# A two-layer decoder trunk: the MLP's down projection with tokens on the partitions, and a changed order of first loads

## The chip, the cores and the metric

One of the eight cores of a Trainium2 chip. The metric is the device time of one execution in microseconds (us), the median of several runs. In the profile PE is TensorE's matmuls, PEld its weight loads, DVE VectorE, ACT ScalarE, POOL GpSimd, SP the engine that only issues DMAs. L155 is line 155 of the kernel before.

## The reference

The trunk has 256 tokens, a model width of 2048, and two layers. Each layer is a mixer and a gated MLP, each behind an RMS norm and with a residual. Layer 0's mixer joins a gMLP (8 head groups) and a gated recurrence (HGRN2, 8 heads); layer 1's is an attention with forget gates (16 heads). The part that the change touches most is the MLP's last product:

```python
def conv_ffn(h, w_up, conv_w, conv_b, w_down):
    z = h @ w_up                                   # (256, 2048) x (2048, 2 * 5632)
    zp = jnp.pad(z, ((0, 0), (CONV_WIDTH - 1, 0), (0, 0)))
    z = sum(conv_w[j] * zp[:, j:j + seq] for j in range(CONV_WIDTH)) + conv_b
    a, b = jnp.split(z, 2, axis=-1)
    return (jax.nn.silu(a) * b) @ w_down           # (256, 5632) x (5632, 2048)

for l in range(DEPTH):
    x = x + mixer(rms_norm(x, mix_norm[l]))
    x = x + conv_ffn(rms_norm(x, ffn_norm[l]), ...)
```

Everything is float32 in and out.

## The kernel before

**Layout.** The residual stream x is held with features on the partitions: 16 tiles xT[m] of 128 features x 256 tokens. All weights stream from memory once, about 430 MB.

**Split products.** Every large product is computed from float32 values cut in two: a high part rounded to the matmul's fast format (fp32r) and the rest. ScalarE makes the high part wh of a weight tile (L139), VectorE the rest wl (L141), from the raw tile w that SP's queue loads (L137); all in weights(). Activations are split likewise by split(): one tile of 512 columns holds 256 columns high, 256 low. A product is high x high + low x high + high x low.

**Two forms of projection.** project() keeps features on the partitions: per weight tile of 128 x 128 one matmul with wh against all 512 columns (L155) and one with wl against the 256 high columns (L158), both into one PSUM bank; fold() or add_x() add the two halves. The argument run says how many weight tiles are taken together before the order changes from wh to wl. project_tok() puts tokens on the partitions: the activation is the stationary operand and 512 columns of weights stream past; three matmuls (L177, L178, L179) per weight tile row and half of the tokens, into two banks. It serves v, i and the attention's q, k, v.

**Small work between.** Generators (hgrn, attend, mixes, gated, spatial, finish) do the recurrence, the attention and other small parts; tick() is called once per weight load and advances every generator in flight by one yield; depth[0] is how many may be in flight (2). They use PSUM banks from px, the projections those of pm. The order of instructions on each engine is written down ahead of time by a list scheduler from the program's order and its dependencies.

**Norm.** feed_split(k) makes the split, gain-scaled tile a of xT[k]; feed_square(k) adds its square to acc. At the kernel's start both run inside the first project_tok, the adds on POOL. Elsewhere feed() does both, on VectorE, right after a tile of x is complete. finish() makes the row factor R.

**Start.** The 2 MB of x come as five parts, the first by SP's queue, four by ScalarE's; the first 100 columns of the parameter array pp come by POOL's queue; WARM matmuls on a tile of ones run meanwhile.

**MLP.** ffn() goes over 4 groups of 11 hidden tiles. up(g) makes a group's 11 activations from 22 projections (conv); down(g) adds the group's product into all 16 tiles of x: per tile m one project() over 11 hidden tiles in chunks of 6 and 5, then add_x. The order is up 0, up 1, down 0, up 2, down 1, up 3, down 2, down 3. In down 3 each finished tile goes to feed() (layer 0) or to the output (layer 1). A second weight pool (fw) makes the buffers deeper during the MLP.

Of the kernel before, what the change touches and what calls it, by code (L numbers as in the profile page):

```python
# [14 lines left out]
P = 128  # L15
# [6 lines left out]
HT = HID // P  # L22
GRP = 11
EPS = 1e-6
WARM = 12
LEVELS = (64, 32, 16, 8, 4, 2, 1)
NL = len(LEVELS)
MCOLS = 2 * (NL + 1) * P
# [16 lines left out]
def tile_trunk(ctx: ExitStack, tc: tile.TileContext, x, pp_d, cst_d, mlev_d, msk_d,  # L45
# [5 lines left out]
    wp = ctx.enter_context(tc.tile_pool(name="wp", bufs=4))  # L51
    apool = ctx.enter_context(tc.tile_pool(name="ap", bufs=KT))
    tp = ctx.enter_context(tc.tile_pool(name="tp", bufs=2))
    pm = ctx.enter_context(tc.tile_pool(name="pm", bufs=3, space=bass.MemoryType.PSUM))
    px = ctx.enter_context(tc.tile_pool(name="px", bufs=1, space=bass.MemoryType.PSUM))

    count = [0]
# [1 line left out]
    def nm(base):  # L59
        count[0] += 1  # L60
        return f"{base}_{count[0]}"

    xT = []
    xload = []
    for c0, n in ((0, 2), (2, 2), (4, 4), (8, 4), (12, 4)):
        t = cp.tile([P, n, S], F32, tag=f"x{c0}", name=f"x{c0}")
        xload.append((t, c0, n))
        xT += [t[:, i] for i in range(n)]
    pp = cp.tile([P, NPP], F32, tag="pp", name="pp")
    cst = cp.tile([P, NK], F32, tag="cst", name="cst")  # L70
    ones = cp.tile([P, P], F32, tag="ones", name="ones")
    one1 = cp.tile([P, 1], F32, tag="one1", name="one1")

    nc.gpsimd.dma_start(pp[:, 0:C_CW], pp_d[:, 0:C_CW])
    V.memset(ones, 1.0)
    V.memset(one1, 1.0)
    ident = cst[:, K_ID:K_ID + P]
# [23 lines left out]
    def bank(tag="px"):  # L101
        n = nm(tag)
        return px.tile([P, 512], F32, tag=tag, name=n, bufs=banks[tag])

    banks = {"px": 5}
    flight, queue = [], []

    def tick():
# [6 lines left out]
    depth = [2]  # L115

    SC.preload_act_table_set(LNEXP)
    for i, (t, c0, n) in enumerate(xload):
        (SC if i else nc.sync).dma_start(t, x[:, c0:c0 + n, :])
    warm = pm.tile([P, 512], F32, tag="pm", name="warm")  # L120
    for i in range(WARM):
        PE.matmul(warm[:, 0:P], ones, ones, start=True, stop=True)
# [1 line left out]
    def drain():  # L124
        while flight or queue:
            tick()

    deep = {"pool": None, "turn": 0}

    def weights(src, n):  # L130
        deep["turn"] += 1
        if deep["pool"] is not None and deep["turn"] > 6 and deep["turn"] % 2:
            pool, nw, ns = deep["pool"], 4, 2
        else:
            pool, nw, ns = wp, 4, 3
        w = pool.tile([P, n], F32, tag="w", name=nm("w"), bufs=nw)
        nc.sync.dma_start(w, src)  # L137
        wh = pool.tile([P, n], F32R, tag="wh", name=nm("wh"), bufs=ns)
        SC.activation(wh, w, AF.Copy)  # L139
        wl = pool.tile([P, n], F32R, tag="wl", name=nm("wl"), bufs=ns)  # L140
        V.tensor_tensor(wl, w, wh.bitcast(F32), ALU.subtract)  # L141
        return wh, wl

    def project(wsrc, acts, chunks=(8, 8), k0=0, run=1):
        ps = pm.tile([P, 512], F32, tag="pm", name=nm("pm"))
        nk = sum(chunks)
        done = 0
        for c in chunks:
            lo = (k0 + done) * P
            tick()  # L150
            wh, wl = weights(wsrc[:, lo:lo + c * P], c * P)
            for k1 in range(0, c, run):
                ks = range(k1, min(k1 + run, c))
                for k in ks:
                    PE.matmul(ps, wh[:, k * P:(k + 1) * P], acts[done + k],  # L155
                              start=done + k == 0, stop=False, skip_group_check=True)
                for k in ks:
                    PE.matmul(ps[:, S:2 * S], wl[:, k * P:(k + 1) * P], acts[done + k][:, 0:S],  # L158
                              start=False, stop=done + k == nk - 1, skip_group_check=True)
            done += c  # L160
        return ps

    def project_tok(wsrc, norm, feed=False):
        ps = [pm.tile([P, 512], F32, tag="pm", name=nm("pm")) for _ in range(2)]
        k = 0
        for c in ((1, 1, 1, 1) + (2,) * 6 if feed else (2,) * 8):
            if feed:
                for i in range(c):
                    norm.feed_split(k + i)
            tick()  # L170
            wh, wl = weights(wsrc[:, k * 512:(k + c) * 512], c * 512)
            for T in range(2):
                for i in range(c):
                    a = norm.a[k + i]
                    ah, al = a[:, T * P:(T + 1) * P], a[:, S + T * P:S + (T + 1) * P]
                    h, l = (t[:, i * 512:(i + 1) * 512] for t in (wh, wl))
                    PE.matmul(ps[T], ah, h, start=k + i == 0, stop=False)  # L177
                    PE.matmul(ps[T], ah, l, start=False, stop=False)  # L178
                    PE.matmul(ps[T], al, h, start=False, stop=k + i == KT - 1)  # L179
            if feed:  # L180
                for i in range(c):
                    norm.feed_square(k + i, nc.gpsimd)
            k += c
        return ps

# [3 lines left out]
        V.tensor_tensor(t, ps[:, 0:S], t, ALU.add)  # L189
        return t  # L190

    def project_norm(wsrc, acts, R, out=None, run=1):
        t = fold(project(wsrc, acts, run=run))
        if out is None:
            out = t
        V.tensor_tensor(out, t, R, ALU.mult)  # L196
        return out
# [72 lines left out]
    def mixer_ab(norm):  # L270
# [10 lines left out]
        gv, late = [], []  # L281

        def finish():
            yield
            late.extend(norm.finish(tok=True))
            yield
            for T in range(2):
                act(gv[0][:, T], gv[0][:, T], AF.Gelu, scale=late[1][:, T:T + 1])
# [14 lines left out]
        A = norm.a  # L303

        SC.dma_start(cst, cst_d)
        wt = hp.tile([P, 2, NH, P], F32, tag="QK", name="wt", bufs=2)
        SC.dma_start(wt[:, 0], spw_d)
        SC.dma_start(wt[:, 1], spb_d.partition_broadcast(P))
        SC.dma_start(pp[:, C_CW:NPP], pp_d[:, C_CW:NPP])
# [63 lines left out]
        for h in range(NH):  # L373
# [9 lines left out]
            lf.append(l)  # L383
            kq.append(t)
        yB = [None] * KT

        itoks = []

        def hgrn(h):
            l, t = lf[h], kq[h]  # L390
            d0 = (h % 4) * P
            SC.activation(l, l, AF.Identity, bias=lb[:, h:h + 1], scale=omlb[:, h:h + 1])
            st = hp.tile([P, 2, P], F32, tag="st", name=nm("st"), bufs=2)
            dg = bank()
            for T in range(2):
                PE.matmul(dg[:, T * P:(T + 1) * P], t[:, T], t[:, 3 - T], start=True, stop=True)  # L396
# [2 lines left out]
            yield  # L399

            V.tensor_tensor(t[:, 2:4], t[:, 2:4], view(l, P, (-P, 2), (1, P)), ALU.mult)
            E = hp.tile([P, NL, 2, P], F32, tag="QK", name=nm("E"), bufs=2)
            tot = l
            for li in reversed(range(NL)):
                n = LEVELS[li]
# [17 lines left out]
            for c0, c1 in ((0, 4), (4, NL)):  # L423
                sps = bank()
                for li in range(c0, c1):
                    PE.matmul(sps[:, (li - c0) * P:(li - c0 + 1) * P],  # L426
                              E[:, li, 0], E[:, li, 1], start=True, stop=True)
                if c0 == 0:
                    xps = bank()
                    PE.matmul(xps[:, 0:P], t[:, 0], t[:, 2], start=True, stop=True)  # L430
                    s128 = hp.tile([P, P], F32, tag="s128", name=nm("s128"), bufs=2)
                    SC.activation(s128, xps[:, 0:P], AF.Copy)
                V.tensor_tensor(smk[:, c0 * P:c1 * P], sps[:, 0:(c1 - c0) * P],
                                msk[:, c0 * P:c1 * P], ALU.mult)
                for li in range(c0, c1):
                    n = LEVELS[li]
                    sv = view(st[:, 1], 0, (2 * n, 64 // n), (n - P, 2), (1, n))
                    V.tensor_tensor(sv, sv, smk[:, li * P:(li + 1) * P].rearrange(
                        "p (b two n) -> p b two n", two=2, n=n), ALU.add)
# [59 lines left out]
        for h in range(NH):  # L499
# [10 lines left out]
            if gates and not (queue or flight):  # L510
                queue.extend(spatial(b, z) for b, z in todo)
                todo = []
        drain()

        nxt = Norm(C_FFN)
        ks = [yB[8 + h] for h in range(NH)] + [yB[h] for h in range(NH)]
        for m in range(KT):
            add_x(m, project(w_abo[m], ks, run=4))
            nxt.feed(m)
        es.close()  # L520
        return nxt
# [2 lines left out]
    def mixer_c(norm):  # L524
# [109 lines left out]
            todo = []  # L634
        nxt = Norm(C_FFN + KT)
        for m in range(KT):
            add_x(m, project(w_co[m], yB, run=4))
            nxt.feed(m)
        es.close()
        return nxt  # L640
# [2 lines left out]
    def ffn(l, norm, last):  # L643
# [5 lines left out]
        nxt = None if last else Norm(C_MIX + KT)  # L649

        def conv(j):
            z = project_norm(w_up[l, j], A, R, run=(2, 8)[l])

            def w(i):
                c = C_CW + (l * 3 + i) * 2 * HT + j
                return pp[:, c:c + 1]

            cb = C_CB + l * 2 * HT + j
            c = hp.tile([P, S], F32, tag="conv", name=nm("conv"), bufs=4)
            SC.activation(c, z, AF.Identity, bias=pp[:, cb:cb + 1], scale=w(2))  # L660
            V.scalar_tensor_tensor(c[:, 1:], z[:, :S - 1], w(1), c[:, 1:], ALU.mult, ALU.add)  # L661
            V.scalar_tensor_tensor(c[:, 2:], z[:, :S - 2], w(0), c[:, 2:], ALU.mult, ALU.add)  # L662
            return c

        def up(g):
# [9 lines left out]
                hid.append(t)  # L675
            return hid

        def down(g, hid):
            for m in range(KT):
                add_x(m, project(w_dn[l, m], hid, chunks=(6, 5), k0=g * GRP, run=(3, 6)[l]))  # L680
                if g == HT // GRP - 1:
                    if last:
                        nc.sync.dma_start(out[:, m, :], xT[m])
                    else:
                        nxt.feed(m)

        hids = [up(0)]
        for g in range(HT // GRP):
# [91 lines left out]
```

## Time and profile before

| | us |
|---|---|
| time, median of 3 runs (2371.09 to 2371.52) | 2371.42 |
| the profiled execution's own time | 2372.19 |
| its span, first to last instruction | 2370.4 |

| engine | busy us | share of the span | instructions |
|---|---|---|---|
| PE | 2360.5 | 100% | 13118 |
| PEld | 2045.7 | 86% | 13118 |
| DVE | 1754.6 | 74% | 2969 |
| ACT | 1324.8 | 56% | 2249 |
| POOL | 16.2 | 1% | 20 |

The costliest groups of instructions, with the mean of one: the weight splits of 128 x 1024 take 1.06 us on ScalarE (640 of them) and 1.23 us on VectorE; those of 128 x 768 and 128 x 640 (the down projection's) 0.85 and 0.74 us on ScalarE, 0.96 and 0.83 us on VectorE. The adds of a 128 x 256 tile on VectorE take 0.41 to 0.43 us, of 128 x 512 0.69 us. The DMA engines were busy 45% to 75% of most stretches, at 185 GB/s on average. The granted clock of TensorE was 0.998 of full speed over the span.

How to read it: busy shares of TensorE count a matmul from its start to its modelled end, and matmuls overlap, so the distance between the starts of neighbours says more than a duration. Idle time of an engine that is not the bottleneck costs nothing.

### The profile page before, as it was taken

The page shows a single profiled execution, that of the slowest core. Times are in us where ns is not written, and L with a number is a line of the kernel's source. Part 1 is how long each engine was busy: PE and PEld are TensorE (multiplying, and loading weights), DVE is VectorE, ACT ScalarE, POOL GpSimd, SP SyncE. Part 2 cuts the span into 40 slices and gives each one's busy share as a digit, 9 for nine tenths or more (in the row PEclk, how much of TensorE's full clock was granted, in tenths as well). Part 3 has the DMA queues.
Part 4 walks back from the last instruction along what each step waited for, and adds up shares of the span by engine and source line. Part 5 has one row for each costly group of instructions (what it writes and reads, how often), then busy time and mean ns, then how long its engine had stood idle before and what let it go on. Part 6 is the DMA issues. An engine that isn't in the chain of part 4 may idle for free.

```text
span 2370.4 us, 35641 instructions
## 1 busy us (share of the span) xinstructions
PE 2360.5 (100%) x13118; PEld 2045.7 (86%) x13118; DVE 1754.6 (74%) x2969; ACT 1324.8 (56%) x2249; POOL 16.2 (1%) x20
## 2 busy tenths in 40 slices
PE   9999999999999999999999999999999999999999
PEld 7888888888888888888888888888888888888888
DVE  7778886878767867867766666767778767767765
ACT  6655665655555555556555455556555555555543
POOL 2000000000000000000000000000000000000000
PEclk9999999999999999999999999999999999999999
DMA  7554455655575566566656554557555575575565
GB/s 259 178 167 153 152 190 202 223 191 190 156 211 198 167 193 206 172 174 187 198 170 182 171 161 167 187 189 238 194 187 187 155 223 189 153 222 189 153 190 145
DMA packets 133727, 439.69 MB, mean 185 GB/s; under 512 B 14865, under 2 KB 16929, under 8 KB 133425
## 3 DMA queue, kind: packets, MB, share of 16 engines
q1 hardware_dynamic: 132224, 433.40, 58.2%
q10 hardware_dynamic: 1296, 3.97, 0.5%
q8 instruction: 104, 1.70, 0.3%
q14 instruction: 71, 0.57, 0.1%
q0 software_dynamic: 32, 0.05, 0.0%
HBM read 435.24 MB, written 2.11 MB: 185 GB/s over the span
## 4 chain that ended last, share of the span: by engine, by line
PE 97%; DVE 2%; ACT 1%; issue 0%; DMA 0%; ACTq 0%; DVEq 0%; POOLq 0%
PE pm L155 53%; PE pm L158 27%; PE pm L178 5%; PE pm L177 5%; PE pm L179 5%; DVE wl L141 1%; PE px L426 1%; PE px L599 0%; PE px L563 0%; PE px L570 0%; DMA pp<-in_pp 0%; PE px L594 0%; DVE a L205 0%; PE px L396 0%; ACT wh L139 0%
## 5 line engine op out<-in xcount | busy, mean ns | idle before, releaser
L141 DVE TENSOR_TENSOR wl<-w,wh 128x1024 fp32r<-128x1024 f32 (+3 forms) x900 | 1015.8, 1129 | 519.2 <-ACT wh L139 513.4
L139 ACT ACTIVATE wh<-w 128x1024 fp32r<-128x1024 f32 (+3 forms) x900 | 883.2, 982 | 904.4 <-PE pm L155 635.1
L155 PE MATMUL pm<-a,wh 128*128 128x512 f32 x3600 | 1074.7, 395 | 0.0
L158 PE MATMUL pm<-a,wl 128*128 128x256 f32 x3600 | 694.5, 281 | 0.0
L155 PEld LDWEIGHTS pm<-a,wh 128*128 128x128 f32 x3600 | 614.9, 189 | 79.4 <-DVE a L205 0.8
L158 PEld LDWEIGHTS pm<-a,wl 128*128 128x128 f32 x3600 | 604.6, 189 | 76.5 <-issue 0.2
L155 PE MATMUL pm<-hid,wh 128*128 128x512 f32 x1408 | 389.0, 394 | 0.0
L155 PEld LDWEIGHTS pm<-hid,wh 128*128 128x128 f32 x1408 | 239.3, 189 | 27.9
L158 PEld LDWEIGHTS pm<-hid,wl 128*128 128x128 f32 x1408 | 219.8, 189 | 33.6
L158 PE MATMUL pm<-hid,wl 128*128 128x256 f32 x1408 | 228.9, 281 | 0.0
L177 PE MATMUL pm<-wh,a 128*128 128x512 f32 x512 | 203.8, 399 | 3.0 <-ACT wh L139 3.0
L178 PE MATMUL pm<-wl,a 128*128 128x512 f32 x512 | 201.9, 394 | 0.9 <-DVE wl L141 0.9
L179 PE MATMUL pm<-wh,a 128*128 128x512 f32 x512 | 201.1, 393 | 0.0
L177 PEld LDWEIGHTS pm<-wh,a 128*128 128x128 f32 x512 | 96.9, 189 | 22.5 <-ACT wh L139 3.2
L178 PEld LDWEIGHTS pm<-wl,a 128*128 128x128 f32 x512 | 96.9, 189 | 21.5 <-DVE wl L141 2.5
L179 PEld LDWEIGHTS pm<-wh,a 128*128 128x128 f32 x512 | 96.8, 189 | 20.0
L660 ACT ACTIVATE conv<-ev,pp 128x256 f32<-128x256 f32 x176 | 103.1, 586 | 18.2 <-DVE ev L196 18.1
L189 DVE TENSOR_TENSOR ev<-pm,ev 128x256 f32<-128x256 f32 x225 | 93.8, 417 | 4.2 <-ACT ev L188 4.2
L661 DVE SCALAR_TENSOR_TENSOR conv<-ev,pp,conv 128x255 f32<-128x255 f32 x176 | 84.2, 478 | 8.7 <-ACT conv L660 8.7
L662 DVE SCALAR_TENSOR_TENSOR conv<-ev,pp,conv 128x254 f32<-128x254 f32 x176 | 85.0, 483 | 6.2
L188 ACT ACTIVATE ev<-pm 128x256 f32<-128x256 f32 x225 | 82.5, 366 | 0.7 <-PE pm L158 0.6
L196 DVE TENSOR_TENSOR ev<-ev,R 128x256 f32<-128x256 f32 x184 | 78.2, 425 | 6.1
(176 smaller groups left out, 1453.5 us busy)
## 6 DMA issues: line engine op xcount, KB each, us to landing
w<-in_w_up SPq DMA_DIRECT2D x352, 512.0 KB, 4.2
w<-in_w_dn SPq DMA_DIRECT2D x128, 384.0 KB, 3.2
w<-in_w_cqkv SPq DMA_DIRECT2D x96, 512.0 KB, 3.7
w<-in_w_dn SPq DMA_DIRECT2D x128, 320.0 KB, 3.3
w<-in_w_abo SPq DMA_DIRECT2D x32, 512.0 KB, 3.5
w<-in_w_cg SPq DMA_DIRECT2D x32, 512.0 KB, 3.8
w<-in_w_co SPq DMA_DIRECT2D x32, 512.0 KB, 3.6
w<-in_w_f SPq DMA_DIRECT2D x16, 512.0 KB, 4.5
```

Of the source, the lines that this page charges most:

```text
L139: SC.activation(wh, w, AF.Copy)
L141: V.tensor_tensor(wl, w, wh.bitcast(F32), ALU.subtract)
L155: PE.matmul(ps, wh[:, k * P:(k + 1) * P], acts[done + k], start=done + k == 0, stop=False, skip_group_check=True)
L158: PE.matmul(ps[:, S:2 * S], wl[:, k * P:(k + 1) * P], acts[done + k][:, 0:S], start=False, stop=done + k == nk - 1, skip_group_check=True)
L177: PE.matmul(ps[T], ah, h, start=k + i == 0, stop=False)
L178: PE.matmul(ps[T], ah, l, start=False, stop=False)
L179: PE.matmul(ps[T], al, h, start=False, stop=k + i == KT - 1)
L188: SC.activation(t, ps[:, S:2 * S], AF.Copy)
L189: V.tensor_tensor(t, ps[:, 0:S], t, ALU.add)
L660: SC.activation(c, z, AF.Identity, bias=pp[:, cb:cb + 1], scale=w(2))
L661: V.scalar_tensor_tensor(c[:, 1:], z[:, :S - 1], w(1), c[:, 1:], ALU.mult, ALU.add)
L662: V.scalar_tensor_tensor(c[:, 2:], z[:, :S - 2], w(0), c[:, 2:], ALU.mult, ALU.add)
```

## The change

1. The down projection. Groups and order stay. For each group the 16 output tiles are taken in four quarters of four tiles. A quarter has tokens on the partitions: two PSUM banks (one per half of the tokens), the hidden activation as stationary operand, and 512 columns of weights, four tiles m side by side, as moving operand, three matmuls per hidden tile and half. A weight load takes two hidden tiles of four m (128 x 1024, the last one of a quarter 128 x 512), in runs of 1 KB instead of 3 and 2.5 KB. The sums are collected over groups in y (128 x 2 x 2048). In the last group turn() transposes y's tiles back, four f32 transposes per bank and eight per quarter, and adds them to x; the last quarter of the last group is done by project() as before.
2. First loads: x in seven parts, each issued beside the k-tile of the first project_tok where FETCH puts it (parts from tile 8 on by ScalarE's queue, the others by SP's); the first 32 columns of pp by SP, ahead of everything, the next 68 by ScalarE after cst; 15 warming matmuls; the first norm's squares leave the first project_tok and go into finish(), on VectorE.
3. run=2 in every project().
4. Three heads in flight in the recurrence (depth 3, one more yield at hgrn's start, own buffers E, three of st and s128); four banks each in pm and px instead of 3 and 5.

```diff
-WARM = 12
+WARM = 15
+FETCH = {0: (0,), 1: (1, 2, 8), 2: (4, 6), 3: (12,)}
...
-    pm = ... bufs=3 ...
+    pm = ... bufs=4 ...
-    for c0, n in ((0, 2), (2, 2), (4, 4), (8, 4), (12, 4)):
+    for c0, n in ((0, 1), (1, 1), (2, 2), (4, 2), (6, 2), (8, 4), (12, 4)):
...
-    nc.gpsimd.dma_start(pp[:, 0:C_CW], pp_d[:, 0:C_CW])
+    nc.sync.dma_start(pp[:, 0:C_FFN], pp_d[:, 0:C_FFN])
...
-    banks = {"px": 5}
+    banks = {"px": 4}
...
-    for i, (t, c0, n) in enumerate(xload):
-        (SC if i else nc.sync).dma_start(t, x[:, c0:c0 + n, :])
...
-    def project(wsrc, acts, chunks=(8, 8), k0=0, run=1):
+    def project(wsrc, acts, chunks=(8, 8), k0=0, run=2):
...  project_tok
             if feed:
+                for c0 in FETCH.get(k, ()):
+                    t, c0, n = fetch[c0]
+                    (SC if c0 >= 8 else nc.sync).dma_start(t, x[:, c0:c0 + n, :])
                 for i in range(c):
                     norm.feed_split(k + i)
...
-            if feed:
-                for i in range(c):
-                    norm.feed_square(k + i, nc.gpsimd)
...  mixer_ab
         def finish():
-            yield
+            for k in range(KT):
+                norm.feed_square(k)
+                if k % 3 == 2:
+                    yield
             late.extend(norm.finish(tok=True))
...
         SC.dma_start(cst, cst_d)
+        SC.dma_start(pp[:, C_FFN:C_CW], pp_d[:, C_FFN:C_CW])
...
+        depth[0] = 3
         def hgrn(h):
+            yield
-            st = ... bufs=2 ...
+            st = ... bufs=3 ...
-            E = hp.tile([P, NL, 2, P], F32, tag="QK", name=nm("E"), bufs=2)
+            E = hp.tile([P, NL, 2, P], F32, tag="E", name=nm("E"), bufs=2)
...
-            add_x(m, project(w_abo[m], ks, run=4))
+            add_x(m, project(w_abo[m], ks, run=2))
...
-            z = project_norm(w_up[l, j], A, R, run=(2, 8)[l])
+            z = project_norm(w_up[l, j], A, R, run=2)
...  ffn
+        y = hp.tile([P, 2, D], F32, tag="y", name=nm("y"))
+        def turn(m0):
+            for m in range(m0, m0 + 4, 2):
+                tps = bank()
+                for i in range(4):
+                    PE.transpose(tps[:, i * P:(i + 1) * P],
+                                 y[:, i % 2, (m + i // 2) * P:(m + i // 2 + 1) * P], ident)
+                for i in range(2):
+                    V.tensor_tensor(xT[m + i], xT[m + i], tps[:, i * S:(i + 1) * S], ALU.add)
+        def finish_x(m):
+            if last:
+                nc.sync.dma_start(out[:, m, :], xT[m])
+            else:
+                nxt.feed(m)
         def down(g, hid):
-            for m in range(KT):
-                add_x(m, project(w_dn[l, m], hid, chunks=(6, 5), k0=g * GRP, run=(3, 6)[l]))
-                if g == HT // GRP - 1:
-                    if last:
-                        nc.sync.dma_start(out[:, m, :], xT[m])
+            final = g == HT // GRP - 1
+            late = []
+            for q in range(4):
+                if final and q == 3:
+                    for m in range(4 * q, KT):
+                        ps = project(w_dn[l, m], hid, chunks=(6, 5), k0=g * GRP, run=2)
+                        if late:
+                            late.pop()()
+                            turn(4 * q)
+                        add_x(m, ps)
+                        finish_x(m)
+                    return
+                ps = [pm.tile([P, 512], F32, tag="pm", name=nm("pm")) for _ in range(2)]
+                for k in range(0, GRP, 2):
+                    c = min(2, GRP - k)
+                    lo = (g * GRP + k) * P
+                    wh, wl = weights(w_dn[l, 4 * q:4 * q + 4, :, lo:lo + c * P]
+                                     .rearrange("m p c -> p m c"), 4 * c * P, 4)
+                    for T in range(2):
+                        for i in range(c):
+                            a = hid[k + i]
+                            ah, al = a[:, T * P:(T + 1) * P], a[:, S + T * P:S + (T + 1) * P]
+                            h, lo_ = (view(t, i * P, (c * P, 4), (1, P)) for t in (wh, wl))
+                            PE.matmul(ps[T], ah, h, start=k + i == 0, stop=False)
+                            PE.matmul(ps[T], ah, lo_, start=False, stop=False)
+                            PE.matmul(ps[T], al, h, start=False, stop=k + i == GRP - 1)
+                    if k == 4 and late:
+                        late.pop()()
+                for T in range(2):
+                    d = y[:, T, q * 512:(q + 1) * 512]
+                    if g == 0:
+                        SC.activation(d, ps[T], AF.Copy)
                     else:
-                        nxt.feed(m)
+                        V.tensor_tensor(d, d, ps[T], ALU.add)
+                if final:
+                    def done(m0=4 * q):
+                        turn(m0)
+                        for m in range(m0, m0 + 4):
+                            finish_x(m)
+                    late.append(done)
```

## The prediction

> **What bounds the kernel now.** I read the page first, then the idle time by waits, then TensorE's own timeline stage by stage, because only that shows what one matmul really takes from start to start.
>
> From the page (parts 1, 4 and 6) and the view of waits:
>
> ```profile
> span 2370.4 us, 35641 instructions
> PE 2360.5 (100%) x13118; PEld 2045.7 (86%) x13118; DVE 1754.6 (74%) x2969; ACT 1324.8 (56%) x2249; POOL 16.2 (1%) x20
> ...
> PE 97%; DVE 2%; ACT 1%; issue 0%; DMA 0%; ACTq 0%; DVEq 0%; POOLq 0%
> ...
> pp<-in_pp POOLq DMA_DIRECT2D x1, 50.0 KB, 6.3
> ```
>
> ```profile
> ACT wh L139 <- PE pm L155: 635.1, 584, 3.1
> ```
>
> TensorE fills 97% of the chain. ScalarE's largest wait is for TensorE to give a weight buffer back, so the weights are made ahead of need. Only two things can move the time: fewer nanoseconds of TensorE issue, or a new hole in its stream. A mean duration (395 ns for a 512-column matmul) is latency; what counts is the distance between starts. Four excerpts of TensorE's timeline (start, us, line, tiles, count):
>
> ```profile
> 1205.20 0.39 PE L177 MATMUL pm<-wh,a 128*128 128x512 f32 x1
> 1205.42 0.39 PE L178 MATMUL pm<-wl,a 128*128 128x512 f32 x1
> 1205.65 0.39 PE L179 MATMUL pm<-wh,a 128*128 128x512 f32 x1
> 1205.88 0.39 PE L177 MATMUL pm<-wh,a 128*128 128x512 f32 x1
> ```
>
> ```profile
> 1700.42 2.00 PE L155 MATMUL pm<-a,wh 128*128 128x512 f32 x8
> 1702.26 1.11 PE L158 MATMUL pm<-a,wl 128*128 128x256 f32 x8
> 1703.21 2.00 PE L155 MATMUL pm<-a,wh 128*128 128x512 f32 x8
> ```
>
> ```profile
> 2250.43 1.55 PE L155 MATMUL pm<-hid,wh 128*128 128x512 f32 x6
> 2251.82 0.88 PE L158 MATMUL pm<-hid,wl 128*128 128x256 f32 x6
> 2252.53 1.32 PE L155 MATMUL pm<-hid,wh 128*128 128x512 f32 x5
> 2253.70 0.76 PE L158 MATMUL pm<-hid,wl 128*128 128x256 f32 x5
> 2254.29 0.40 PE L155 MATMUL pm<-hid,wh 128*128 128x512 f32 x1
> ```
>
> ```profile
> 1216.08 1.03 PE L563 MATMUL px<-cst,z 128*128 128x128 f32 x8
> 1216.87 0.48 PE L177 MATMUL pm<-wh,a 128*128 128x512 f32 x1
> 1217.19 0.40 PE L178 MATMUL pm<-wl,a 128*128 128x512 f32 x1
> ```
>
> First: with tokens on the partitions (project_tok) a 512-column matmul starts every 227 ns. Second and third: with features on the partitions (project) a weight tile costs one 512- and one 256-column matmul: (1703.21-1700.42)/8 = 349 ns in the up projection, (2254.29-2250.43)/11 = 351 ns here; over whole down groups (61.65 us for 176 pairs in each of four) 350.3 ns. At 227 ns per 512 columns those 768 columns would take 340. Fourth: eight f32 transposes take 0.79 us and the next matmul runs 0.09 us late, 0.88 in all.
>
> **The change, part by part**, against the profiled execution: 2372.19 us, a span of 2370.4 and 1.8 around it, 0.8 above the median of 2371.42.
>
> Down projection. Per four output tiles and one hidden tile, 4 x 350.3 = 1401 ns become 6 matmuls x 227 = 1360 ns. Of 1408 (m,k) pairs the last quarter of the last group of each layer (2 x 44) stays as it was, so 1320 x (350.3-340) = **-13.6 us**. No row shows a moving operand in four runs of 128 columns at a stride, as these weight views are. Two 256-column matmuls (113 to 120 ns each) cost about one of 512, so a break has no fixed price there: I take 227. The other end is 233, the start distance of 512-column matmuls inside project, which leaves no gain.
>
> Transposes. Four calls of turn() per layer, eight transposes each: 8 x 0.88 = **+7.0 us** on TensorE, with nothing to hide them (ends 6.4, at 0.8 per turn, and 8).
>
> The Trainium skill (TensorE: Matmul & The Clock Gate, Part 4) says that transposes do not count as activity for the full clock. If so, 0.8 us of them every 15 us could cost clock; the attention stage, which holds such bursts, kept a granted clock of 1.00, so the trace does not bear out a price.
>
> VectorE and ScalarE in the down groups. Per quarter VectorE has 5 x 1.23 + 0.69 (splits) + 2 x 0.69 (adds into y) = 8.2 us against TensorE's 15.0; before it was 4 x (1.78+0.84) = 10.5. Cost nothing. In layer 0's last group feed() and turn() come in bursts of four tiles: 8.2 + 4 x (0.42+0.98) = 13.8 of 15.0, and at the last four tiles 4 x 3.6 + 5.6 + 1.7 = 21.7 us of VectorE against 17 of TensorE. Five split buffers (10 us of work) cover part; what is late is the last normalised tile, for which the next projection already waited a little. **+1 us** (0 to 5). The two last turn() calls need four px banks, and there are four.
>
> Weight loads of the down groups are 512 KB in 1 KB runs instead of 384 and 320 KB in 3 and 2.5 KB runs, one per 12 x 227 = 2.72 us (193 GB/s). The 2064 packets of 1024 B in this trace (mostly the output stores) took 46.8 ns on average: 512 x 46.8 / 16 = 1.5 us per load. Hidden; if not, see the first rival.
>
> Runs of two. Layer 0's up projection already has run=2: 348.3 ns per pair (122.61 us for 352). Layer 1's (run 8) takes 349.2, w_co (4) 350.8, w_abo (4) 353.4. Run 1 falls at 346.7 or 353.8, by stretch. To 348.3: 1408 x 0.9 + 256 x 2.5 + 256 x 5.1 = 3.2; the 784 pairs of run 1 about 1 (w_cg alone sits at 353.8). As w_abo's price may come from its tiles, not its run, I take **-3.6** (+1 to -5).
>
> Start. The first real matmul starts at 8.65 us, because pp comes by the POOL queue at 1.23 + 6.3, and then a split (0.51) and wh (0.61) follow. Two stretches (busy and count of PE, PEld, DVE, ACT, POOL; clock; DMA share; GB/s):
>
> ```profile
> 8.65:14.80 6.15, 6.15 (x15) 4.75 (x16) 5.82 (x10) 5.46 (x13) 2.91 (x3) 0.50 1.00 361
> 14.80:34.40 19.60, 18.75 (x80) 14.46 (x79) 19.01 (x19) 17.00 (x32) 12.39 (x12) 1.00 0.64 185
> ```
>
> In the first TensorE had half its clock after an idle 3 us, and the DMA engines were full; in the second VectorE was, slowed by the squares on POOL (a split of 0.86 beside POOL, 0.48 without). After: pp is first on SP (16 KB by SP took 3.6 us elsewhere, so 4.3), x0 one and w0 two issues of 0.4 behind it; w0 at about 5.5, first matmul about 6.2, where 30 warming matmuls end. x1 and x2 go ahead of w1 on SP, x4 and x6 ahead of w2, two 512 KB parts on ScalarE's queue. Up to w3 that is 3.1 MB, 8.5 us at 361 GB/s, so TensorE still waits at k=1 to 3 and has four of 16 k-tiles by about 13; the other 72 matmuls take 16.3 us: end near 30 instead of 34.4. The 16 squares and 15 adds (16 x 0.40 ScalarE, 15 x 0.42 VectorE) move to the second w_v half, where VectorE has some 7 us free of 23. Should the clock halve again, 2.7 is lost. **-3.5** (-1.5 to -5). The rest of pp moves behind cst on ScalarE's queue and is read after that half: nothing.
>
> Three heads. Between 112 and 315 us TensorE has a dozen waits beyond its rhythm, some 3.5 us. Arrival is one head per four ticks and a head lasts about ten, so three in flight match; two E buffers and four px banks can bite. **-1** (-3 to +3). pm=4 frees nothing that waited.
>
> Sum: -13.6 + 7.0 + 1 - 3.6 - 3.5 - 1 = **-13.7**: 2358.5 for a profiled run, 2358 beside the median. A measurement of this kernel can tell 0.2%, 4.7 us.
>
> **Rivals.** (A) The loads become the bound, slower. It decides when a 1 KB packet costs over 2.72 x 16 / 512 = 85 ns. The 640 packets of 2 KB took 105 ns on average with waiting included; if packets get no cheaper than that, a load lasts 3.35 us, 0.63 too long, on 165 chunks: +104, 2462. For it: 22 KB between rows and 2.9 MB between the four blocks, a pattern no row has, and 4 KB packets averaged 199 ns where 159 was typical. Against: 46.8 ns per 1 KB, and 361 GB/s at the start. 0.06. The Trainium skill (DMA: Bandwidth & Descriptors, Latency and other measured facts) gives 207 down to 103 GB/s for row pitches of 512 KiB to 4 MiB; no run here shows such a pitch, and 164 GB/s by that page would add some 80 us, an estimate.
>
> (B) The strided moving operand brings 233 ns: the 13.6 is gone, 2372, no change. 0.07.
>
> (C) The projection gains, but VectorE's burst at layer 0's end (+5) and the heads (+3) take back 6 to 8: 2365, still faster. 0.12.
>
> (D) Start or heads go wrong by more than 10 us altogether, slower or level: 0.05.
>
> **Numbers.** Forecast 0.70, C 0.12, B 0.07, A 0.06, D 0.05. The low ends of all terms at once give 2372.2 - 20.2 - 0.8 = 2351; all high ends at once would give 2373, about half of that excess 2366, and C lies at 2365: 2351 to 2368. Faster by over 0.2% (below 2366.7): 0.84; within: 0.08; slower: 0.08.
>
> **What would show it.** Matmuls of the down groups 227 ns apart (233 or holes after wh: B or A); 64 transposes in eight bursts of 0.8 us; a quarter of a group 15.0 us long; DMA share there below 0.9 (A: at 1.0, with waits of ScalarE on w_dn); first real matmul near 6.2 us; layer 1's up projection at 348.3; no hole over 2 us where w_cf follows layer 0's MLP. A down group longer than 61.65 us makes the forecast wrong.

## The result, and the profile after

The changed kernel takes 2358.92 us (median of 4 runs, 2358.37 to 2359.36); the kernel before took 2371.47 on the same chip (4 runs, 2371.09 to 2371.54). The ratio is 0.9946, 95% interval 0.9932 to 0.9960: faster by 12.6 us. The forecast was 2358.0. The profiled execution took 2359.05 us, a span of 2357.2 and 1.85 around it.

The lines of the page after that answer to those shown of before (span, part 1, the chain, part 6):

```profile
span 2357.2 us, 33532 instructions
PE 2348.7 (100%) x12528; PEld 2011.1 (85%) x12528; DVE 1689.0 (72%) x2760; ACT 1286.3 (55%) x2085; POOL 0.2 (0%) x4
...
PE 99%; DMA 0%; ACT 0%; DVE 0%; SPq 0%; issue 0%; ACTq 0%
...
w<-in_w_dn SPq DMA_DIRECT2D x150, 512.0 KB, 3.6
```

TensorE's share of the chain went from 97 to 99%: VectorE's 2% and ScalarE's 1% are gone. POOL has lost its squares. The down projection's new loads land 3.6 us after their issue, like most of the other weights (3.5 to 3.7 at the median; the up projection's 4.2).

TensorE's timeline in a down group (the matmuls of L727 to L729, start and duration in us), and the stretch of one whole down group, before and after, in the view by windows (stretch, length, then busy us and count of PE, PEld, DVE, ACT, POOL; granted clock; DMA share; GB/s):

```profile
700.29 0.39 PE L727 MATMUL pm<-wh,hid 128*128 128x512 f32 x1
700.51 0.39 PE L728 MATMUL pm<-wl,hid 128*128 128x512 f32 x1
700.74 0.39 PE L729 MATMUL pm<-wh,hid 128*128 128x512 f32 x1
```

```profile
651.54:713.19 61.65, 61.65 (x354) 53.89 (x353) 42.97 (x68) 31.59 (x51) 0.00 (x0) 1.00 0.74 211
```

```profile
647.90:707.77 59.87, 59.87 (x267) 49.57 (x265) 28.94 (x31) 27.99 (x35) 0.00 (x0) 1.00 0.59 197
```

The starts are 227 ns apart and the group has no hole: 264 matmuls of 227 ns are 59.9 us. The DMA share fell to 0.59. ScalarE's largest waits are still for TensorE to give a buffer back; the loads are not late:

```profile
ACT wh L139 <- PE pm L155: 473.1, 392, 2.9
ACT wh L139 <- PE pm L729: 248.7, 169, 2.8
```

Where the time went, from the starts of each stage's first matmul in the two timelines (us):

| stage | before | after | difference |
|---|---|---|---|
| up to w_f's first matmul (the start and w_v) | 57.87 | 55.77 | -2.10 |
| w_f | 53.80 | 53.72 | -0.08 |
| recurrence (i, q, g, u) | 203.18 | 201.87 | -1.31 |
| w_abo | 90.82 | 90.66 | -0.16 |
| layer 0: up | 491.10 | 491.08 | -0.02 |
| layer 0: down | 246.61 | 243.34 | -3.27 |
| w_cf and q, k, v | 295.84 | 295.60 | -0.24 |
| w_cg | 98.12 | 97.19 | -0.93 |
| w_co | 89.80 | 89.45 | -0.35 |
| layer 1: up | 492.29 | 491.09 | -1.20 |
| layer 1: down | 246.77 | 243.51 | -3.26 |
| behind the last matmul | 4.16 | 3.97 | -0.19 |

The sum is -13.1. Half of it is the down projection.

### The profile page after: what moved, and what is told of

It is laid out like the page before. It is cut to its first block, busy times and chain, and to the rows that moved or that the text cites. A ratio compares the mean times of both kernels' runs of the same rounds, so it can differ in the third digit from the quotient of the medians.

```text
span 2357.2 us, 33532 instructions
## 1 busy us (share of the span) xinstructions
PE 2348.7 (100%) x12528; PEld 2011.1 (85%) x12528; DVE 1689.0 (72%) x2760; ACT 1286.3 (55%) x2085; POOL 0.2 (0%) x4
## 4 chain that ended last, share of the span: by engine, by line
PE 99%; DMA 0%; ACT 0%; DVE 0%; SPq 0%; issue 0%; ACTq 0%
PE pm L155 42%; PE pm L158 21%; PE pm L728 6%; PE pm L727 6%; PE pm L729 6%; PE pm L181 5%; PE pm L182 5%; PE pm L180 5%; PE px L432 1%; DMA w<-in_w_v 0%; PE px L606 0%; PE px L692 0%; PE px L570 0%; PE px L577 0%; PE px L601 0%; PE px L402 0%
## 5 line engine op out<-in xcount | busy, mean ns | idle before, releaser
L141 DVE TENSOR_TENSOR wl<-w,wh 128x1024 fp32r<-128x1024 f32 (+1 forms) x840 | 1004.3, 1196 | 556.2 <-ACT wh L139 553.9
L139 ACT ACTIVATE wh<-w 128x1024 fp32r<-128x1024 f32 (+1 forms) x840 | 871.1, 1038 | 962.2 <-PE pm L155 473.1
L155 PE MATMUL pm<-a,wh 128*128 128x512 f32 x3600 | 1135.3, 396 | 0.0
L158 PEld LDWEIGHTS pm<-a,wl 128*128 128x128 f32 x3600 | 676.1, 188 | 158.9
L158 PE MATMUL pm<-a,wl 128*128 128x256 f32 x3600 | 708.7, 278 | 0.0
L155 PEld LDWEIGHTS pm<-a,wh 128*128 128x128 f32 x3600 | 549.6, 189 | 1.5 <-DVE a L205 0.8
L727 PE MATMUL pm<-wh,hid 128*128 128x512 f32 x660 | 257.1, 390 | 0.0
L728 PE MATMUL pm<-wl,hid 128*128 128x512 f32 x660 | 256.8, 389 | 0.0
L729 PE MATMUL pm<-wh,hid 128*128 128x512 f32 x660 | 256.8, 389 | 0.0
L729 PEld LDWEIGHTS pm<-wh,hid 128*128 128x128 f32 x660 | 123.9, 188 | 25.7
L727 PEld LDWEIGHTS pm<-wh,hid 128*128 128x128 f32 x660 | 123.9, 188 | 25.5
L728 PEld LDWEIGHTS pm<-wl,hid 128*128 128x128 f32 x660 | 123.9, 188 | 25.3
```

Of the source, the lines that this page charges most:

```text
L155: PE.matmul(ps, wh[:, k * P:(k + 1) * P], acts[done + k], start=done + k == 0, stop=False, skip_group_check=True)
L728: PE.matmul(ps[T], ah, lo_, start=False, stop=False)
L729: PE.matmul(ps[T], al, h, start=False, stop=k + i == GRP - 1)
```

## The experiments

**The four parts, each alone on the kernel before** (10 runs each, all on one chip; before there 2371.42, 31 runs, 2370.19 to 2374.36).

The down projection alone:

```diff
-                add_x(m, project(w_dn[l, m], hid, chunks=(6, 5), k0=g * GRP, run=(3, 6)[l]))
+            for q in range(4):
+                ... (as in the change, with run=(3, 6)[l] kept for the last quarter of the last group)
```

> The kernel before with the new down projection alone (loads, transposes, y); runs, banks, first loads and heads as before. Theory (the parts add, each at its own stage): six groups without transposes at 59.85 us instead of 61.65, two last groups 2.1 us longer, together -6.5 us: 2365 us. Rival 1 (the loads in 1 KB runs or VectorE's bursts need the four pm banks of the full change): groups longer than 61.65 us, 2371 or more. Rival 2 (the parts help each other): less than 4 us gained.

Measured: 2366.25 us (2364.31 to 2367.18), ratio 0.9978 [0.9969, 0.9988]: -5.2 us. The down stages of its profile are 243.37 and 243.62 us against 246.61 and 246.77 before: -6.4 in all, close to the -6.5 expected. The profiled run, 2364.31, is the fastest of the ten and 1.9 below their median; what the others lost stands in no trace. Two stages whose code is as before moved too: w_cg took 96.91 us here (98.12 before) and w_cf with q, k and v 295.60 (295.84), while the recurrence stayed (203.20 and 203.18).

The first loads alone:

```diff
+FETCH = {0: (0,), 1: (1, 2, 8), 2: (4, 6), 3: (12,)}
...  (pp first on SP, x in seven parts, WARM = 15, the squares in finish())
```

> The kernel before with the new first loads alone (x in seven parts, pp first on SP, 15 warming matmuls, squares in the second half). Theory: -2.1 us, as the stages of the changed kernel show: no stretch at half clock (2.7 us gained), first matmul 1.2 us earlier, and new waits of TensorE for the first weight tiles (about 1.6, 1.5 and 0.5 us) that take part of it back: 2369.3 us. Rival (the step of the prediction, VectorE relieved of POOL and earlier weights): -3.5 us, 2368.

Measured: 2370.70 us (2369.21 to 2372.53), ratio 0.9998 [0.9989, 1.0007]: -0.7, not to be told from nothing. In its profile the first matmul starts at 6.67, 2 us sooner than before, and w_f at 56.08 instead of 57.87. TensorE's timeline shows where the early start is spent (a hole, here and below, is the distance between the starts of the two matmuls around it):

```profile
10.53 0.40 PE L182 MATMUL pm<-wh,a 128*128 128x512 f32 x1
12.59 1.22 PE L180 MATMUL pm<-wh,a 128*128 128x512 f32 x2 [1.67 <-ACT wh L139]
13.61 0.63 PE L181 MATMUL pm<-wl,a 128*128 128x512 f32 x1
14.04 0.63 PE L182 MATMUL pm<-wh,a 128*128 128x512 f32 x1
```

After the second weight tile there is a hole of 2.07 us, because the third has not come; from there on a matmul takes 0.63 instead of 0.40 us and starts are 430 ns apart. The windows view gives that stretch a clock of 0.50:

```profile
12.60:16.00 3.40, 3.40 (x8) 2.68 (x9) 2.89 (x6) 3.15 (x7) 0.00 (x0) 0.50 0.90 304
```

Runs of two alone (run=2 in every project(), the down projection included):

```diff
-    def project(wsrc, acts, chunks=(8, 8), k0=0, run=1):
+    def project(wsrc, acts, chunks=(8, 8), k0=0, run=2):
-            add_x(m, project(w_abo[m], ks, run=4))
+            add_x(m, project(w_abo[m], ks, run=2))
-            z = project_norm(w_up[l, j], A, R, run=(2, 8)[l])
+            z = project_norm(w_up[l, j], A, R, run=2)
...  (and w_co, w_dn likewise)
```

> The kernel before with run=2 in every project and nothing else. Theory: layer 1's up projection -1.2 us, w_co -0.4, w_cg -0.9, the other stages of run 1 -0.5, w_abo still 353 ns per pair: together about -3 us, 2368.4. Rival (w_abo falls to 348 when the other parts are left out): -4.3 us, 2367.2. Second rival (a pair's price is set by what runs beside it, not by run): below 1 us.

Measured: 2366.71 us (2366.27 to 2368.35), ratio 0.9980 [0.9971, 0.9990]: -4.7. The recurrence gives 1.3 (201.87 us), w_cg 0.9, layer 1's up projection 1.2, w_co 0.4. w_abo stays at 353 ns per pair, so it is not the first rival that brings the time near its 2367.2. The down groups fall to 61.42, 349.0 ns per pair, a gain that the changed kernel has only in its last quarters. Stage by stage this kernel and the changed one agree within 0.1 us in w_f, recurrence (to 0.00), w_abo, w_cg, w_co and layer 1's up projection.

Three heads in flight alone:

```diff
+        depth[0] = 3
         def hgrn(h):
+            yield
...  (tags and buffers as in the change, pm 4 and px 4 banks)
```

> The kernel before with three heads in flight, own buffers E and four banks each in pm and px. Theory: TensorE's waits in the recurrence fall by about 1 us and nothing else moves: 2370.5 us. Rival 1 (the 1.3 us that this stage gained in the changed kernel are run=2's alone): 2371.4, no change. Rival 2 (four px banks hold the attention back): slower by 1 us or more between 1150 and 1440 us.

Measured: 2371.14 us (2370.20 to 2372.34), ratio 0.9999 [0.9990, 1.0009]: nothing to be told. In the profile the recurrence is 0.9 us shorter (202.29). Layer 0's down groups, whose code is untouched, are shorter as well (61.44 us instead of 61.65), so it does not hold that nothing else moves.

The four alone sum to -5.2 - 0.7 - 4.7 - 0.3 = -10.9 us; the change brings -12.6 on one chip and -9.3 on another (below).

**What the transposes cost.** The changed kernel without turn()'s body; it leaves out that y is added to x:

```diff
         def turn(m0):
-            for m in range(m0, m0 + 4, 2):
-                ...
+            pass
```

> The changed kernel without the transposes: turn() does nothing, so y is computed but not added to x (all of the down product except the last quarter of the last group is missing from the output). Theory (TensorE pays each burst of eight in full, 0.88 us, and nothing hides it): 8 x 0.88 = 7.0 us less, 2351.9 us, the last group of each layer at 60.1 us instead of 63.7. Rival (part of a burst lies beside waits, or VectorE's adds behind it set the pace): less than 5 us or more than 9 us.

Measured: 2353.89 us (2352.87 to 2356.49, 4 runs), ratio 0.9930 [0.9913, 0.9946]; before on that chip 2371.53 (7 runs). The total is 2.0 above the 2351.9 expected: in its profile (2352.88) w_f began at 56.63 us instead of 55.77, behind a hole of 2.34 us. The stages are therefore compared. Layer 0's last two groups (down 2 and down 3, which follow each other without a break), in the changed kernel and in this one (windows):

```profile
1012.82:1136.44 123.62, 123.62 (x584) 103.56 (x583) 79.34 (x117) 59.25 (x84) 0.00 (x0) 1.00 0.54 164
```

```profile
1013.65:1133.73 120.08, 120.08 (x552) 100.11 (x551) 70.27 (x91) 53.38 (x68) 0.00 (x0) 1.00 0.57 172
```

32 instructions and 3.54 us less; layer 1 gives 3.56. So 64 transposes cost 7.1 us, 111 ns each, and the clock is 1.00 either way. One burst in the changed kernel:

```profile
2312.45 1.03 PE L692 MATMUL px<-cst,y 128*128 128x128 f32 x8
2313.24 0.48 PE L727 MATMUL pm<-wh,hid 128*128 128x512 f32 x1
2313.56 0.40 PE L728 MATMUL pm<-wl,hid 128*128 128x512 f32 x1
```

0.79 us for eight, and the next matmul's successor 0.09 later than 227 ns.

**Whether the loads come near to being the bound.** The changed kernel with one hidden tile per weight load, which halves the runs to 512 B and the loads to 256 KB:

```diff
-                for k in range(0, GRP, 2):
-                    c = min(2, GRP - k)
+                for k in range(GRP):
+                    c = 1
```

> The changed kernel with one hidden tile per weight load in the down quarters: 256 KB in runs of 512 B, one load per 1.36 us, so a packet of 512 B may take 1.36 x 16 / 512 = 42.5 ns before the loads bind (85 ns for the 1 KB runs of the change). Theory (the DMA engines have room: packets of 1024 B took 46 ns at the median and 52 on average in the changed kernel, of 512 B 27 and 28): down groups stay at 59.85 us, the total within 1 us, plus at most what twice as many, shorter splits cost VectorE and ScalarE, which is hidden. Rival (the loads are near their limit): groups of 62 us and more, waits of ScalarE on w_dn, total over 2365.

Measured: 2363.36 us (one run, which a start with a hole of 4.96 us explains: w_f began at 60.06). The down groups last 59.85 us, as with 1 KB runs. In a down group (windows):

```profile
652.00:711.00 59.00, 59.00 (x263) 48.88 (x262) 32.90 (x49) 33.09 (x53) 0.00 (x0) 1.00 0.72 214
```

Twice the packets cost a DMA share of 0.72 instead of 0.59 and no time. A 512 B packet took 27 ns and a 1 KB packet 46 (medians, 28.4 and 52.4 on average), where the first rival needed 85 for 1 KB. With one hidden tile per load the 512 columns also lie in one piece, not in four runs at a stride, and the group lasts the same 59.85 us: the stride costs nothing.

**What the heads bring beside runs of two.** The changed kernel with two heads in flight:

```diff
-        depth[0] = 3
         def hgrn(h):
-            yield
...  (E, st, s128, pm and px as before)
```

> The changed kernel with two heads in flight, three pm and five px banks, and the buffers of before. Theory (run=2 alone took the slack of the recurrence: 203.2 us fell to 201.9 with it alone, to 202.3 with the three heads alone, to 201.9 with both): no change, within 0.5 us, 2358.9. Rival 1 (the heads bring their 0.9 us also beside run=2): slower by about 1 us. Rival 2 (fewer pm banks stall the down quarters, which take two at once): slower by 2 us or more there.

Measured: 2361.88 us (2359.93 to 2363.18, 4 runs), ratio 0.9959 [0.9944, 0.9974]. That is 3.0 above the 2358.9 expected, but not by the heads: in its profile (2361.20) w_f began at 57.88 us, 2.1 later than in the changed kernel, behind a hole of 3.87 us. The recurrence by windows, before, in this kernel and in the changed one:

```profile
111.67:314.84 203.17, 202.78 (x1159) 174.23 (x1158) 164.01 (x425) 126.02 (x307) 0.00 (x0) 1.00 0.49 159
```

```profile
111.60:313.46 201.86, 201.63 (x1158) 173.81 (x1157) 164.48 (x426) 125.91 (x308) 0.00 (x0) 1.00 0.50 160
```

```profile
109.49:311.36 201.87, 201.74 (x1159) 173.70 (x1157) 164.46 (x427) 125.73 (x307) 0.00 (x0) 1.00 0.48 162
```

Two heads or three: 201.9. The slack that three heads take (0.9 alone) is the slack that runs of two take. The starts show the same: behind project()'s 512-column matmuls this stage had 8 distances of over 350 ns before, 1 with runs of two alone, 3 with the heads alone and 3 with both.

**The start.** In the changed kernel, TensorE's timeline and the DMA issues of SP's queue begin so:

```profile
7.50 0.73 PE L180 MATMUL pm<-wh,a 128*128 128x512 f32 x2 [1.36 <-ACT wh L139]
...
11.38 0.40 PE L182 MATMUL pm<-wh,a 128*128 128x512 f32 x1
12.88 0.73 PE L180 MATMUL pm<-wh,a 128*128 128x512 f32 x2 [1.10 <-ACT wh L139]
```

```profile
3.06 0.43 SPq L137 DMA_DIRECT2D w<-in_w_v  x1
3.68 2.30 SPq L170 DMA_DIRECT2D x<-in_x  x2
6.81 1.71 SPq L137 DMA_DIRECT2D w<-in_w_v  x3
```

The third weight tile is issued only at 6.81, though SP has nothing else to do. The trace names what it waits for: this program's transfers take eight semaphores in turn, both queues together, and an issue waits until the transfer that had its semaphore before, the one eight back in the program's order, has landed. So x4 goes out at 3.68 behind pp's landing at 3.66, x6 at 5.65 behind x0's at 5.64, and the third w at 6.81 behind the first w's at 6.80; the fourth w follows it on the queue at 7.19. Each early part of x, and each transfer on ScalarE's queue, takes one of the eight turns and so puts off a weight tile; the third landed at 12.2 us here, at 11.8 to 15.0 in the other profiles of this order. Its issue differs little between them (6.0 to 6.8); its transfer took 5.4 to 8.4 us, with 256 to 512 KB parts of x under way beside it, and why it is longer in some runs is open. A first attempt to mend it put fewer and larger parts of x on SP's queue alone:

```diff
-FETCH = {0: (0,), 1: (1, 2, 8), 2: (4, 6), 3: (12,)}
+FETCH = {0: (0,), 1: (1,), 3: (4,), 4: (8,), 6: (12,)}
...
-    for c0, n in ((0, 1), (1, 1), (2, 2), (4, 2), (6, 2), (8, 4), (12, 4)):
+    for c0, n in ((0, 1), (1, 3), (4, 4), (8, 4), (12, 4)):
...
-                    (SC if c0 >= 8 else nc.sync).dma_start(t, x[:, c0:c0 + n, :])
+                    nc.sync.dma_start(t, x[:, c0:c0 + n, :])
```

> The changed kernel with x in five parts of 1, 3, 4, 4, 4 tiles, all on SP's queue, put between the first weight loads in order of need. Theory (the start lost to two things: a new transfer was issued only when an older one, eight before it, had landed, so w for the third k-tile went out at 6.8 us; and 512 KB of late x shared the engines with the first weights): first matmul before 6.2 us, no wait over 0.5 us after it, the first projection of w_f at 52 us or earlier instead of 55.8: 3 to 4 us less, 2355.5 us. Rival (ScalarE's and VectorE's splits set the pace of the first tiles): less than 1 us gained.

Measured: 2362.20 us (2361.23 to 2362.87, 4 runs), ratio 0.9961 [0.9946, 0.9976]: no gain. The hole after the second tile is gone, but with x off ScalarE's queue the constants cst (256 KB) and the rest of pp move up on it and are issued at 0.76 and 5.86 us; the holes are now at 14 and 18 us, and again half a clock follows (start of the matmul at 18.96, 0.63 us long):

```profile
14.12 0.50 PE L181 MATMUL pm<-wl,a 128*128 128x512 f32 x1 [1.20 <-DVE wl L141]
...
18.25 0.50 PE L181 MATMUL pm<-wl,a 128*128 128x512 f32 x1 [1.68 <-DVE wl L141]
...
18.96 0.63 PE L180 MATMUL pm<-wh,a 128*128 128x512 f32 x1
```

The last two were run together (before on that chip 2370.94, 9 runs, 2369.98 to 2373.09): the changed kernel as it is, and one with everything of the start on SP's one queue, in the order in which it is needed.

> The changed kernel once more, unedited, beside the next one. Theory (all stages behind the first 60 us repeat to 0.1 us; the start does not, since the third weight tile is issued late and TensorE's wait for it was 1.1 to 4.7 us, and since a clock window in which TensorE is busy a third of the time or less is followed by one at half clock): between 2358 and 2363.5, median near 2361, the first projection of w_f between 55.5 and 60.1 us. Rival (the four runs at 2358.4 to 2359.4 are typical): 2358.9.

Measured: 2361.65 us (2359.39 to 2362.92, 5 runs), ratio 0.9960 [0.9947, 0.9974]. In its profiled run, the fastest, the hole is 1.85 us long and no clock is lost. Of the nine runs of the changed kernel on the two chips, the five with a mean granted clock of 1.000 took 2358.4 to 2359.4 us, the four with 0.999 took 2361.2 to 2362.9; all four of the first chip are of the first kind.

```diff
-FETCH = {0: (0,), 1: (1, 2, 8), 2: (4, 6), 3: (12,)}
+FETCH = {0: (0,), 1: (1,), 3: (4,), 6: (8,), 10: (12,)}
...  (x in parts of 1, 3, 4, 4, 4, all by SP)
-        SC.dma_start(cst, cst_d)
+        nc.sync.dma_start(cst, cst_d)
...  (likewise the rest of pp, wt and kst)
```

> The changed kernel with every load of the first 60 us on SP's queue in the order of need: x in parts of 1, 3, 4, 4, 4 tiles, the third and fourth weight tile ahead of the late x, and cst, pp's rest, wt and kst behind the weights instead of on ScalarE's queue. Theory: no hole over 0.6 us after the first matmul and no stretch at half clock; the first projection of w_f at 52 to 53 us; 2355.5 us, and a narrower spread than the changed kernel's. Rival 1 (the DMA engines' rate, some 310 GB/s for 6.3 MB, sets the first half): holes move to later tiles as in the run with reordered x, no gain, 2360 to 2362. Rival 2 (the masks and wt come too late for the mixes): a new hole in the w_f stage, which then takes over 54.5 us instead of 53.7.

Measured: 2358.10 us (2357.80 to 2358.75, 5 runs), ratio 0.9945 [0.9932, 0.9957]. Its slowest run is below the fastest of the changed kernel beside it; the medians are 3.55 us apart. The start by windows and on the timeline:

```profile
5.95:14.50 8.55, 7.45 (x30) 4.57 (x29) 7.56 (x16) 7.88 (x19) 0.00 (x0) 1.00 1.01 393
```

```profile
5.95 0.48 PE L180 MATMUL pm<-wh,a 128*128 128x512 f32 x1
...
8.11 0.73 PE L180 MATMUL pm<-wh,a 128*128 128x512 f32 x2 [0.34 <-ACT wh L139]
...
12.09 0.50 PE L181 MATMUL pm<-wl,a 128*128 128x512 f32 x1 [0.24 <-DVE wl L141]
...
14.38 0.50 PE L181 MATMUL pm<-wl,a 128*128 128x512 f32 x1 [0.53 <-DVE wl L141]
```

TensorE begins at 5.95 (7.50 in the first profile of the changed kernel, 6.81 in the one beside), its longest wait up to 14.5 us is 0.53, and the DMA engines are full (1.01, 393 GB/s): up to there the limit is the bytes, of which another order could bring no more. w_f begins at 53.88, 1.9 sooner than in the changed kernel and not at 52 to 53 as expected; 0.9 of that is lost again in w_f (54.66 us instead of 53.72, more than the second rival's 54.5), with small holes at 59.7 and 62.9 us. So the kernel beats the changed one beside it, by making every run as good as the best: all five had a granted clock of 1.000, and the ratio, 0.9945, is that of the changed kernel's four runs on the first chip (0.9946). The 2355.5 expected was missed by 2.6. One queue and the order of need were changed together here; which of them brings how much is not shown.

## Why the prediction was right, and where its terms were not

The forecast of 2358.0 was met within a microsecond on the first chip, by a sum whose large terms held and whose small ones partly cancelled. That it came so close was luck: on another chip the same kernel took 2361.65, still faster than before by 9.3 us and inside the range, but 3.7 above the forecast. As far as profiles and clocks show, the difference lies in the start, whose hole is longer in some runs than in others.

- **Down projection and transposes, -13.6 and +7.0.** Held, each by itself. Without transposes the down stages fell by (246.61 - 239.80) + (246.77 - 239.97) = 13.6 us; the transposes cost 7.1; with both, 6.5 was left against 6.6 of the sum. The choice of 227 ns for the strided moving operand was right: four runs of 128 columns stream as fast here as one of 512.
- **VectorE's burst at layer 0's end, +1.** The step failed: w_cf with q, k and v took 295.60 us against 295.84, and w_cf itself 6.99 against 7.16. The burst cost TensorE nothing; that the split buffers cover all of it is likely, but was not tried.
- **Runs of two, -3.6.** Measured -4.0, but by other shares. Layer 1's up projection was sized right (-1.2 for 1.27) and w_co too high (-0.35 for 0.64). w_abo's 1.3 was wrong: -0.16 in the changed kernel and the same alone; at run 2 as at run 4 it stays at some 353 ns per pair, so that its price is not the run's (the prediction had left that open). The stages of run 1, sized at 1, brought 2.3: 1.3 in the recurrence, 0.9 in w_cg, 0.1 in w_f. That w_cg's 0.9 belongs to the run is not shown, as the down projection alone lowered it by 1.2.
- **Three heads, -1.** Alone 0.9 in the recurrence, beside runs of two nothing. The step failed by counting the same slack twice: TensorE's waits in the recurrence were given to the heads, and a projection that leaves other gaps takes them first.
- **Start, -3.5.** The mis-sized term: -2.1 in the profiled run, -0.7 as the median of ten runs alone. The first matmul came at 7.50, not 6.2, since the first weight tile landed at 6.80 and not at 5.5 (at 6.0 to 6.6 in the other profiles of this start): the bytes of x's late parts, on ScalarE's queue from 0.76 us, travel beside it. With that queue empty it landed at 4.94, with the 256 KB of constants on it at 5.83. The prediction counted the DMA engines' bytes for the third tile, and left out that SP could not issue it before another transfer had landed. So the first 24 matmuls (four k-tiles) were done at 16.0 us instead of 13, against 17.1 before; the other 72 took 17.0, near the 16.3 of the sum and 1.0 less than before. w_f began at 55.7 to 60.1 us in the profiles of kernels with this start, against 57.8 to 57.9 before. The 2.7 us that half a clock was to cost did not show: the four profiles with the old start spent one or two windows of 3.4 us at half clock, and w_f began within 0.13 us of the same time.
- **Rivals.** The loads as the bound fell by the 59.87 us of a group, and with margin by the 512 B runs. The Trainium skill (DMA: Bandwidth & Descriptors, Latency and other measured facts) gives lower rates for row pitches at large powers of two, from 512 KiB on. No run here has such a pitch: rows 22 KB apart in blocks 2.9 MB apart streamed at 214 GB/s in 512 B runs with the engines at 0.72. The strided operand at 233 ns fell by the starts, and by the group of the same length with the columns in one piece. VectorE's burst and the heads took nothing back. The start did not cost 10 us, but it is where the runs differ.
- **The range.** Its upper end rests on "all high ends at once" as 2373. That sum leaves out the projection's own other end, no gain; with it the high ends come to 2387.
- **Transposes and the clock.** The Trainium skill (TensorE: Matmul & The Clock Gate, Part 4) says that a transpose does not count as busy in the same way as a matmul. Bursts of 0.8 us in streams of matmuls left the granted clock at 1.00, as the prediction took it; bursts so short leave most of a window of 3.4 us to matmuls, so this does not test what the page says.

## What to carry to other kernels

Where TensorE bounds, count the distance between matmul starts of each form in the trace and multiply: 0.227 us per 512 columns against 0.350 per pair gave a term of 13.6 us to within 0.1, and the transposes that pay for it to within 0.1 as well. A gain that is read from waits (the heads here) must not be added to another that closes the same waits. At a kernel's start, put all first loads on one queue in the order of need and follow what each issue waits for: sooner is worth nothing if the third tile comes later, and a long hole brings half a clock on top.

## What the runs showed of the hardware

- **The clock after a hole.** Half-clock stretches begin and end on a grid of 3.413 us, whose phase is another one in each run. The Trainium skill (TensorE: Matmul & The Clock Gate, Part 1) has a free-running window of about 3.4 us; the traces agree. Across the traces, windows at full clock in which TensorE streamed 0.06 to 0.36 of the time (counted from the starts; nine windows) were followed by half a clock, those with 0.37 and more were not. So a hole of 1.50 or 1.85 us passed at full clock here, and one of 2.07 us cost a window. The threshold is read across runs, and was not tried by itself.
- **The way back.** A window at half clock in which TensorE streamed only for the last 1.9, 2.1 or 2.7 us (the 512 B runs, the heads alone, the kernel before) was followed by a second one at half clock; one filled from its beginning was followed by full clock, in all nine traces with half a clock at the start. This too is read across runs.
- **What half a clock costs.** For matmuls without a wait a window at half clock would cost 1.7 us, an estimate: half of its 3.4. In the changed start most of that lies beside waits for weights: from the thirteenth matmul, the first behind the hole, to w_f's first it took 42.9 and 43.3 us without a window at half clock, 43.5 with one (three profiles), 44.4 with two. The length of the hole, 1.50 to 4.96 us, makes more of the difference between runs than the clock.
- **Pair prices lock in.** The 512- and 256-column matmuls of project() settle into repeating patterns, and a stage keeps one: 346.7 or 353.8 ns per pair at run 1, 348.3 to 349.4 at run 2, w_abo some 353 at either run. w_cg, at run 1, went from 98.12 to 96.91 us (from 353.8 to 346.7 ns per pair) when only the down projection was changed. What chooses the pattern is open.
